# Context tokens as the stationary operand of the first FFN's matmuls, with 512 weight columns moving, in a one-layer hybrid mLSTM / spatial-gating kernel

## The chip, the cores and the metric

The kernel runs on one core of one Trainium2 chip. The metric is the device time of one execution in microseconds, as the median of several runs. Before the change it was 2650.72 us (three runs, 2648.93 to 2655.58).

The engines are called by the profile's names: PE multiplies matrices (one operand is held in the array, the other moves through it column by column), PEld loads the held operand, DVE and ACT work elementwise, POOL does a few small things, and SP issues the transfers. Each engine runs its instructions in the order in which they were put on it.

## The reference, cut to what matters

One layer works on 1024 latent tokens and 256 context tokens of width 1024. Both run through a half-step SwiGLU FFN of inner width 2816, a token-mixing part and a second FFN; the context tokens are needed only up to the mixing part.

```
def ffn_sublayer(h, shift, scale, gate, g, w_in, w_out):
    hn = modulate(rmsnorm(h, g), shift, scale)
    a, b = jnp.split(hn @ w_in, 2, axis=-1)      # 1024 -> 2 x 2816
    y = (jax.nn.silu(a) * b) @ w_out             # 2816 -> 1024
    return h + 0.5 * gate[:, None, :] * y
```

Behind the first FFN the mixing part projects the normalised tokens with one wide matrix into q, k, v, gates, o, u and others. It runs a bidirectional mLSTM of four heads over chunks of 128 tokens (whose weights hold `exp(dm - m_t)`) and a chunked spatial-gating MLP, `gelu(u)` times a 128x128 mix of the normalised `gelu(vs)`, merges the two by sigmoid gates and projects once more. Everything is fp32.

## The kernel before, in words

**Numbers and tiles.** Each fp32 operand of a large product is split into a high part (rounded to the type fp32r) and a low part (the remainder): ACT casts the high part and DVE subtracts it from the source (`split`, L145 and L146). A product is then three matmuls: high by high, high by low, low by high (`mm3`, L182). Tokens lie along the free dimension, channels along the partitions: eight tiles of 128 channels by 512 latent tokens (`h`, two token blocks) or by 256 context tokens (`hc`; normalised and split `hnc`).

**Stages.** The latent matrices use a scheme of seven half-size products in place of eight, with pages `fa`, `fb`, `fc` of combined operands. In order of time: adaLN rows (to about 37 us); the first FFN's up-projection of the context tokens (to 169); the same for the latent tokens, `A.gate` with L411 (to 588); the latent down-projection `A.outp` with L535 (to 801); the context down-projection with L1161 (to 867); `wv` by `Rows` (L1292, PSUM tile `pr`) and the context's v (`pvc`, L1451); further projections (`pq`, L1373), with the spatial-gating mix (`pm` by PE, `mx` by DVE, L1813 and L1815) and the Gelu of u among the last; four heads (from about 1577) beside the product with `w_b` (`pt`, L1853); `w_a` and `w_o`; the second FFN (2001 to the end).

**Context up-projection.** `for f in range(NF)` takes two pages of weights per f, one of the SiLU half and one of the other. Weights are held in PE, 256 context tokens move: `pa` and `pb` each take 24 matmuls of 256 columns per f. After two f, ACT takes the SiLU of `pa` (128x512), DVE multiplies by `pb`, ACT and DVE split the result, and SP stores it to DRAM (`gcsp`). The result already has channels on the partitions, as the down-projection wants it. Beside it run the position embedding, the sums of squares of the latent norm (`acc`, L209) and, from f = 10, the scaling of the latent tokens (`inplace`, L261 on DVE and L262 on ACT). At the end `A.begin` loads and splits the gate's first four weight pages into `ring`.

**Context down-projection.** Per f, each of eight channel tiles takes three matmuls of 256 columns with `wring` weights held and `gc` moving, added up in four PSUM tiles `pc`. Then DVE adds the gated result to `hc`, and the next norm of the context tokens follows: ACT squares, DVE adds (`acc`), PE sums over the partitions (`p`, L214), DVE and ACT take the inverse root (`rs_x` to `rs_y`, L758 to L764), ACT and DVE form a diagonal matrix split in two (`diag`, L224 and L225), and PE spreads it (`rb`, L230).

**What sets the order.** The order on PE, DVE and ACT is set by the program's own order and a scheduler below it. Small work is put between matmuls by hand: `todo` is a queue of functions, and `pump` takes one after each 512 columns of matmul (a `nop` there is an empty slot of 512 columns). `tc.issue_after` makes instructions come behind a named one. Weight pages and `ring` tiles live in pools: a page can be overwritten only when its last matmul is done. `ring` has four slots, so the cast of the fifth page waits for the first page's 12 matmuls, and so on.

## Time and profile before

| | us |
|---|---|
| median of three runs | 2650.72 |
| lowest, highest | 2648.93, 2655.58 |
| the profiled execution | 2650.17 |
| its span in the trace | 2648.4 |
| PE busy | 2634.0 (99%), 12904 instructions |
| DVE busy | 1946.5 (73%) |
| ACT busy | 1205.5 (46%) |
| granted PE clock, mean | 0.998 |

The span is the time from the first to the last instruction in the trace; the profiled execution's own time is 1.8 us longer. A busy PE counts the records of matmuls, which overlap: a record lasts longer than the slot that the matmul takes in a stream, so prices per matmul are read from the distance between starts, or from the chain of waits, which gives unbroken pieces with their counts.

### The profile page before, as it was taken

The page shows a single profiled execution, that of the slowest core. Times are in us where ns is not written, and L with a number is a line of the kernel's source. Part 1 is how long each engine was busy: PE and PEld are TensorE (multiplying, and loading weights), DVE is VectorE, ACT ScalarE, POOL GpSimd, SP SyncE. Part 2 cuts the span into 40 slices and gives each one's busy share as a digit, 9 for nine tenths or more (in the row PEclk, how much of TensorE's full clock was granted, in tenths as well). Part 3 has the DMA queues.
Part 4 walks back from the last instruction along what each step waited for, and adds up shares of the span by engine and source line. Part 5 has one row for each costly group of instructions (what it writes and reads, how often), then busy time and mean ns, then how long its engine had stood idle before and what let it go on. Part 6 is the DMA issues. An engine that isn't in the chain of part 4 may idle for free.

```text
span 2648.4 us, 35940 instructions
## 1 busy us (share of the span) xinstructions
PE 2634.0 (99%) x12904; PEld 2211.2 (83%) x12904; DVE 1946.5 (73%) x3490; ACT 1205.5 (46%) x2171; POOL 80.3 (3%) x158
## 2 busy tenths in 40 slices
PE   9999999999999999999999999999999999999998
PEld 6998888888889878888888888888888888888887
DVE  7988688687989646787664869777568766665755
ACT  5664444444346525564443454333256444344433
POOL 0000000000000000000000003221000000000000
PEclk9999999999999999999999999999999999999999
DMA  9834344368578222356653457547341343337654
GB/s 315 307 111 136 119 163 167 113 232 308 175 238 292 74 80 91 104 176 195 197 171 105 150 195 265 184 152 267 129 146 41 124 142 112 123 123 275 202 157 181
DMA packets 201234, 452.73 MB, mean 171 GB/s; under 512 B 20320, under 2 KB 54624, under 8 KB 201056
## 3 DMA queue, kind: packets, MB, share of 16 engines
q1 hardware_dynamic: 200624, 450.05, 50.4%
q8 instruction: 101, 1.65, 0.3%
q14 instruction: 77, 0.63, 0.1%
q10 hardware_dynamic: 432, 0.39, 0.0%
HBM read 329.11 MB, written 121.32 MB: 170 GB/s over the span
## 4 chain that ended last, share of the span: by engine, by line
PE 94%; DMA 2%; issue 2%; ACT 1%; DVE 1%; SPq 0%; POOL 0%; POOLq 0%; DVEq 0%; ACTq 0%
PE qa L411 18%; PE pq L1373 17%; PE po L535 14%; PE qb L411 14%; PE pt L1853 10%; PE pr L1292 5%; PE pa L182 2%; PE pb L182 2%; PE pc L1161 2%; PE pn L1987 2%; PE pu L1695 1%; PE pkc L1352 1%; PE pn L1985 1%; PE pvc L1451 1%; DMA adapg<-in_w_ada_dram 1%
## 5 line engine op out<-in xcount | busy, mean ns | idle before, releaser
L146 DVE TENSOR_TENSOR ring<-rawq,ring 128x512 fp32r<-128x512 f32 x408 | 281.0, 690 | 222.1 <-ACT ring L145 218.7
L535 PE MATMUL po<-gring,wring 128*128 128x512 f32 (+1 forms) x1896 | 424.0, 384 | 0.8 <-DMA gring<-fsp 0.8
L535 PEld LDWEIGHTS po<-gring,wring 128*128 128x128 f32 x1896 | 349.3, 188 | 71.5 <-ACT h L262 1.6
L145 ACT CAST ring<-rawq 128x512 fp32r<-128x512 f32 x408 | 253.3, 622 | 310.4 <-PE pq L1373 88.8
L411 PE MATMUL qa<-fc,ring 128*128 128x512 f32 x1056 | 252.3, 389 | 0.0
L411 PEld LDWEIGHTS qa<-fc,ring 128*128 128x128 f32 x1056 | 198.1, 188 | 41.5 <-DVE fc L146 0.4
L1373 PE MATMUL pq<-fc,ring 128*128 128x512 f32 x864 | 207.6, 392 | 0.0
L145 ACT CAST wring<-rw 128x512 fp32r<-128x512 f32 x154 | 95.7, 622 | 215.4 <-PE po L535 186.0
L1373 PEld LDWEIGHTS pq<-fc,ring 128*128 128x128 f32 x864 | 161.5, 188 | 33.4
L1853 PE MATMUL pt<-yp,ring 128*128 128x512 f32 x768 | 186.9, 396 | 2.3 <-DVE mx L1813 2.3
L1853 PEld LDWEIGHTS pt<-yp,ring 128*128 128x128 f32 x768 | 143.5, 189 | 31.1 <-issue 2.5
L146 DVE TENSOR_TENSOR wring<-rw,wring 128x512 fp32r<-128x512 f32 x154 | 105.6, 686 | 79.9 <-ACT wring L145 79.6
L1373 PE MATMUL pq<-fa,ring 128*128 128x512 f32 x576 | 142.4, 395 | 0.0
L1373 PE MATMUL pq<-fb,ring 128*128 128x512 f32 x576 | 138.5, 394 | 0.0
L1373 PEld LDWEIGHTS pq<-fb,ring 128*128 128x128 f32 x576 | 107.6, 188 | 23.9 <-issue 0.2
L411 PE MATMUL qa<-fa,ring 128*128 128x512 f32 x528 | 127.0, 390 | 0.0
L411 PE MATMUL qb<-fb,ring 128*128 128x512 f32 x528 | 126.5, 389 | 0.0
L411 PE MATMUL qa<-fb,ring 128*128 128x512 f32 x528 | 126.5, 390 | 0.0
L411 PE MATMUL qb<-fc,ring 128*128 128x512 f32 x528 | 126.2, 389 | 0.0
L411 PE MATMUL qb<-fa,ring 128*128 128x512 f32 x528 | 126.2, 389 | 0.0
L1373 PEld LDWEIGHTS pq<-fa,ring 128*128 128x128 f32 x576 | 106.8, 188 | 22.4 <-DVE ring L146 0.2
L793 DVE SCALAR_TENSOR_TENSOR adacc<-adapg,sc,adacc 128x512 f32<-128x512 f32 x154 | 111.9, 747 | 16.8 <-DMA adapg<-in_w_ada_dram 15.7
(364 smaller groups left out, 4652.8 us busy)
## 6 DMA issues: line engine op xcount, KB each, us to landing
adapg<-in_w_ada_dram SPq DMA_DIRECT2D x144, 256.0 KB, 3.6
fsp<-fhl SPq DMA_DIRECT2D x66, 512.0 KB, 2.7
gring<-fsp SPq DMA_DIRECT2D x66, 512.0 KB, 4.1
raw<-in_w1i_dram SPq DMA_DIRECT2D x44, 512.0 KB, 5.2
graw<-fsp SPq DMA_DIRECT2D x88, 256.0 KB, 3.7
rawq<-in_w1i_dram SPq DMA_DIRECT2D x38, 512.0 KB, 3.6
rawq<-in_w2i_dram SPq DMA_DIRECT2D x38, 512.0 KB, 3.6
fsp<-p SPq DMA_DIRECT2D x66, 256.0 KB, 2.2
```

Of the source, the lines that this page charges most:

```text
L145: hi = S.copy(hl[:, 0, :], src)
L146: return hi, V.tensor_sub(hl[:, 1, :], src, hl[:, 0, :].bitcast(F32))
L182: T.matmul(pt, x, y, start=first and i == 0, stop=i == n - 1, skip_group_check=True)
L411: T.matmul(pt, hl[:, x, sl], pages[p][k][:, y, :], start=first and i == 0, stop=i == 11, skip_group_check=not first)
L535: T.matmul(pt[:, cs], w[:, x, sl], g[:, y, cs], start=grp and kp == 0 and i == 0, stop=kp == NFP - 1 and i == 2, skip_group_check=not grp)
L793: eng.scalar_tensor_tensor(acc, pgt, sc2[:, q, k:k + 1], acc, ALU.mult, ALU.add)
L1161: T.matmul(pt, hl[d // 4][:, x, sl], g[:, y, :], start=f == 0 and d % 2 == 0 and i == 0, stop=f == NF - 1 and i == 2, skip_group_check=True)
L1292: T.matmul(self.pt[m], pg[:, x, sl], hl[:, y, :], start=first and k == 0 and i == 0, stop=k == 3 and i == 2, skip_group_check=not first)
L1352: T.matmul(self.cp[:, o:o + 256], hl[:, x, k * 128:(k + 1) * 128], hnc[kc][:, y, :], start=p == 1 and k == 0 and i == 0, stop=p in (2, 4) ...
L1373: T.matmul(pt, hl[:, x, k * 128:(k + 1) * 128], pg[k][:, y, :], start=first and k == 0 and i == 0, stop=k == 3 and i == 2, skip_group_chec ...
L1853: T.matmul(pt, hl[:, x, k * 128:(k + 1) * 128], pg[:, y, :], start=kh + k + i == 0, stop=kh == 1 and k == 3 and i == 2)
L1987: T.matmul(pn[:, 0:257], qi[:, c_, :], self.C[d][:, c_, :], start=False, stop=c_ == 1)
```

## The change

Four things change.

1. *Context up-projection.* The tokens are held and the weights move. A new layout `w1c` of the same weights has 44 pages of 128x1024, four for each of 11 blocks; a page holds two k tiles of 512 columns, of which 256 are of the SiLU half and 256 of the other. Per block, each of two token halves (`pts[0]`, `pts[1]`) takes 24 matmuls of 512 columns. `gated` takes two SiLU of 128x256 and two products; `turned` transposes the result with four PE transposes into `ptg`, splits it from there and stores it. `turned` of a block runs one page into the next block; the last is put into the gate's queue. The old work beside f is in `beside`. The scaling of the second latent block moves to the gate's queue, whose lead goes from 16 to 24.
2. *Context down-projection.* The `gc` tokens are held and 512 columns of `wring` move: 12 matmuls per f in place of 24 narrow ones. ACT and DVE copy the four `pc` to `co`; `cturn`, four times, transposes four tiles into `pct`, and DVE adds them to `hc` from there. `cturn` is queued in `todo` behind three empty slots and so runs inside `wv`.
3. *The latent down-projection.* `A.outp` gets `free`: late loads go to pages that are no longer used. In `fin1` seven empty slots, where three were, stand between the inverse root and the spread.
4. *The heads.* The first head's two exponentials are taken out of `Head` preparation into `expo`, which is issued behind the last Gelu; the split of the `w_b` operand (`yp`) is also tied behind a `mx`.

```diff
-    W = Weights([("w1i", f, 1024) for f in range(2 * NF)], "w1")
+    W = Weights([("w1c", i, 1024) for i in range(4 * NFP)], "w1")
...
-            for d in range(NKT):
-                slow(n1[1].inplace, d, s0, b0)
...
-            for pt, w_ in ((pa, wa), (pb, wb)):
-                proj(pt[:, f % 2 * 256:f % 2 * 256 + 256], w_, hnc, f % 2 == 0 and ks[0] == 0, ks)
...
+    def gated(pts, fn=None):
+        sil = t2("sil").rearrange("p (i c) -> p i c", i=2)
+        for i in range(2):
+            S.activation(sil[:, i, :], pts[i][:, 0:256], AF.Silu)
+        with ExitStack() as es:
+            if fn is not None:
+                es.enter_context(tc.issue_after(fn().ins))
+            for i in range(2):
+                V.tensor_mul(sil[:, i, :], sil[:, i, :], pts[i][:, 256:512])
+        return sil
+
+    def turned(blk, sil):
+        pt = sm_ps("ptg")
+        for j in range(2):
+            for i in range(2):
+                T.transpose(pt[:, j * 256 + i * 128:j * 256 + (i + 1) * 128], sil[:, i, j * 128:(j + 1) * 128], ident)
+        g = [t2("gc", F32R) for _ in range(2)]
+        S.copy(g[0], pt)
+        V.tensor_sub(g[1], pt, g[0].bitcast(F32))
...
+    for blk in range(NFP):
+        pts = [mm_ps("pa") for _ in range(2)]
+        for kp in range(4):
+            if kp % 2 == 0:
+                beside(2 * blk + kp // 2)
+            w_ = W.take("w1c", 4 * blk + kp)
+            for k in (2 * kp, 2 * kp + 1):
+                o = k % 2 * 512
+                for i in range(2):
+                    for n, (x, y) in enumerate(THREE):
+                        T.matmul(pts[i], hnc[k][:, x, i * 128:(i + 1) * 128], w_[:, y, o:o + 512],
+                                 start=k == 0 and n == 0, stop=k == NKT - 1 and n == 2)
+                    pump(512)
+            if kp == 0:
+                if turn is not None:
+                    turned(*turn)
...
+        turn = blk, gated(pts, first_ring if blk == NFP - 1 else None)
+    todo.extend([nop] * 4 + [it(turned, *turn)])
...
-    A.gate(A.F.late(fpage, lambda k: []), tick, 16)
+    A.gate(A.F.late(fpage, lambda k: [it(n1[1].inplace, k, s0, b0)]), tick, 24)
...
-        todo.extend([nop] * 6 + [n_.rstd, nop, nop, nop, n_.bcast])
+        todo.extend([nop] * 6 + [n_.rstd] + [nop] * 7 + [n_.bcast])
...
+           free=(lambda: ringpg("wring"), lambda kp: hnpage(1, "gring") if kp > 3 else ringraw("gring")))
...
+        for i in range(2):
+            for j in range(2):
+                for n, (x, y) in enumerate(THREE):
+                    T.matmul(pcs[2 * i + j], g[:, x, i * 128:(i + 1) * 128], hl[j][:, y, :], start=f == 0 and n == 0,
+                             stop=f == NF - 1 and n == 2)
+                pump(512)
...
+    def cturn(d2):
+        pt = sm_ps("pct")
...
+    todo.extend([nop] * 3)
+    for d2 in range(4):
+        slow(cturn, d2)
...
-            S.activation(pg, pg, AF.Exp)
...
+    with tc.issue_after(ureads[False].ins):
+        for d in range(2):
+            heads[0].expo(d)
```

What this does to the order on the engines, at three places.

ACT at the end of the context up-projection, before; `hl` are casts of its weight pages, `fb` and `h` work for the latent tokens, `sil` the SiLU of the last block, `ring` the casts of the gate's first weights:

```order
L145 CAST hl<-raw 128x1024
L1060 CAST gc<-sil 128x512
L145 CAST hl<-raw 128x1024
L145 CAST fb<-h 128x512 x3
L1052 ACTIVATE sil<-pa 128x512
L145 CAST ring<-rawh 128x512 x5
L1060 CAST gc<-sil 128x512
```

and with the change, where `gc<-ptg` is the high part of a transposed block:

```order
L145 CAST hl<-raw 128x1024
L1051 CAST gc<-ptg 128x512
L145 CAST fb<-h 128x512
L262 ACTIVATE h<-h,mods 128x512 x2
L145 CAST fb<-h 128x512 x2
L1037 ACTIVATE sil<-pa 128x256 x2
L145 CAST ring<-rawh 128x512 x4
```

In both, the last block's SiLU stands directly ahead of the gate's casts; it was one of 512 columns and is now two of 256, which need all of the block's matmuls.

PE at the start of `wv`, before; `pc` is the end of the context down-projection, `p` the sums of the context's norm, `rb` its spread, `pr` the products of `wv`:

```order
L1161 MATMUL pc<-gc,wring 128x256 x456
L1292 MATMUL pr<-ring,fa 128x512 x21
L214 MATMUL p_8226<-ones,acc 128x1 x2
L1292 MATMUL pr<-ring,fa 128x512 x24
L230 MATMUL rb<-diag,onesr 128x256
L1292 MATMUL pr<-ring,fa 128x512
L230 MATMUL rb<-diag,onesr 128x256
L1292 MATMUL pr<-ring,fa 128x512 x50
```

and with the change, where `pct` are the transposes of the down-projection's result (the last `pc` end just ahead of these rows):

```order
L1332 MATMUL pr<-ring,fa 128x512 x15
L1209 MATMUL pct<-cst,co 128x128 x4
L1332 MATMUL pr<-ring,fa 128x512 x6
L1209 MATMUL pct<-cst,co 128x128 x4
L1332 MATMUL pr<-ring,fa 128x512 x6
L1209 MATMUL pct<-cst,co 128x128 x4
L1332 MATMUL pr<-ring,fa 128x512 x6
L1209 MATMUL pct<-cst,co 128x128 x4
L1332 MATMUL pr<-ring,fa 128x512 x15
L214 MATMUL p_7581<-ones,acc 128x1 x2
L230 MATMUL rb<-diag,onesr 128x256 x2
L1332 MATMUL pr<-ring,fa 128x512 x48
```

The sums moved from behind 21 matmuls of `pr` to behind 48 (15 + 6 + 6 + 6 + 15), and between the sums and the spread, where 24 matmuls stood, there is none.

ACT at the same place, before; `ring` are casts of weight pages, `rs_z` the root, `diag` the diagonal, `rx` the copies of the first product that must be made before PE may add the second one there:

```order
L145 CAST ring<-raw_8169 128x512
L760 ACTIVATE rs_z<-rs_x 128x2
L145 CAST ring<-raw_8171 128x512
L145 CAST ring<-raw_8173 128x512
L1526 CAST wgp<-wgr 128x8x16
L224 ACTIVATE diag<-cst,rs_y 128x128 x2
L1303 COPY rx<-pr 128x512 x2
L243 ACTIVATE nt<-nt,mods 128x256
L1303 COPY rx<-pr 128x512
L244 CAST hnc<-nt 128x256
L1303 COPY rx<-pr 128x512
L145 CAST ring<-raw_8175 128x512
```

and with the change:

```order
L1202 COPY co<-pc 128x512 x2
L145 CAST ring<-raw_7431 128x512
L145 CAST ring<-raw_7433 128x512
L1564 CAST wgp<-wgr 128x8x16
L205 ACTIVATE acc<-hc 128x256
L208 ACTIVATE sq<-hc 128x256 x7
L145 CAST ring<-raw_7435 128x512
L145 CAST ring<-raw_7437 128x512
L760 ACTIVATE rs_z<-rs_x 128x2
L224 ACTIVATE diag<-cst,rs_y 128x128 x2
L1343 COPY rx<-pr 128x512 x4
```

The root and the diagonal now stand behind the fourth weight page's cast (`raw_7437`), where they stood ahead of the fourth (`raw_8175`), and all four copies come behind the diagonal.

ACT around the first head's exponentials, before; `P` are the first head's weights, L1931 their exponential, `ug` the Gelu, `yp` the casts of the operand of `w_b`:

```order
L1931 ACT_TABLE_LOAD
L1931 ACTIVATE P<-P 128x1024
L1929 ACTIVATE P<-P,colpg 128x128
L1433 ACT_TABLE_LOAD
L1433 ACTIVATE ug<-ug 128x512
L1931 ACT_TABLE_LOAD
L1931 ACTIVATE P<-P 128x1024
L145 CAST yp<-ld 128x512 x4
L145 CAST ring<-rawt 128x512
L1966 CAST kh<-ptk 128x512
L1430 ACT_TABLE_LOAD
L1430 ACTIVATE ug<-pq 128x512
```

and with the change, where L1976 is the exponential:

```order
L1967 ACTIVATE P<-P,colpg 128x128 x16
L1472 ACTIVATE ug<-ug 128x512
L145 CAST yp<-ld 128x512 x4
L1470 ACTIVATE ug<-pq 128x512
L145 CAST yp<-ld 128x512 x2
L145 CAST ring<-rawt 128x512
L145 CAST yp<-ld 128x512 x2
L145 CAST ring<-rawt 128x512
L1472 ACTIVATE ug<-ug 128x512
L1976 ACT_TABLE_LOAD
L1976 ACTIVATE P<-P 128x1024 x2
```

Both exponentials moved behind the casts of `yp` and the last Gelu, and three of the four table loads shown before are gone.

More of the change, by code (lines that the diff above doesn't have):

```diff
@@ L1014, in slow, with beside @@
         todo.append(f)
-    for f in range(NF):
+    def beside(f):
         if 0 < f <= NKT:
@@ L1034, in _build @@
             A.preload()
-        wa = W.take("w1i", 2 * f)
-        wb = W.take("w1i", 2 * f + 1)
-        if f % 2 == 0:
-            pa, pb = mm_ps("pa"), mm_ps("pb")
-        for ks in (range(6), (6, 7)) if f == 0 else (range(NKT),):
-            for pt, w_ in ((pa, wa), (pb, wb)):
-                proj(pt[:, f % 2 * 256:f % 2 * 256 + 256], w_, hnc, f % 2 == 0 and ks[0] == 0, ks)
-                if f == 0 and ks[0] == 0 and pt is pa:
+    def gated(pts, fn=None):
[8 more added lines that the diff above has]
+        return sil
@@ new lines, in first_ring @@
+    def first_ring():
+        flush()
+        W.c.close()
+        A.begin()
+        return A.q.last[1]
+    turn = None
+    for blk in range(NFP):
[14 more added lines that the diff above has]
+                    turned(*turn)
+                else:
@@ L1043, in _build @@
                     last0()
-                if ks[-1] == NKT - 1:
-                    W.done()
-        if f == 0:
+            W.done()
+        if blk == 0:
             order.close()
-        if f % 2 == 0:
-            continue
-        with ExitStack() as es:
-            sil = t2("sil")
-            S.activation(sil, pa, AF.Silu)
-            if f == NF - 1:
-                flush()
-                W.c.close()
-                A.begin()
-                es.enter_context(tc.issue_after(A.q.last[1].ins))
-            V.tensor_mul(sil, sil, pb)
-            g = [t2("gc", F32R) for _ in range(2)]
-            S.copy(g[0], sil)
-            V.tensor_sub(g[1], sil, g[0].bitcast(F32))
```

51 lines of the change are left out of this document (29 added, 22 removed).

## The prediction

> **What bounds the kernel now.** I read the page's busy shares first, then PE's list of waits, then the chain of waits with its times, then the stretches that the change touches.
>
> ```profile
> PE 2634.0 (99%) x12904; PEld 2211.2 (83%) x12904; DVE 1946.5 (73%) x3490; ACT 1205.5 (46%) x2171; POOL 80.3 (3%) x158
> PE pt L1853 <- DVE mx L1813: 2.3, 1, 2.3
> PE po L535 <- DMA gring<-fsp: 0.8, 2, 0.5
> PE rb L230 <- ACT diag L224: 0.6, 1, 0.6
> 50.69 2.88 PE pa L182 x24
> 245.14 5.44 PE qa L411 x24
> 812.42 54.72 PE pc L1161 x456
> 50.50:169.00 118.50, 118.50 (x983) 118.04 (x982) 107.83 (x163) 81.96 (x118) 0.00 (x0) 1.00 0.75 257
> 108.30:119.80 11.50, 11.50 (x98) 11.50 (x97) 11.49 (x15) 10.15 (x15) 0.00 (x0) 1.00 0.80 265
> ```
>
> PE is busy for 2634.0 of the span's 2648.4 us: 14.4 us are idle in all, and the list of waits names the few that are long. So PE's own stream is the bound nearly everywhere, a transfer or a slow engine costs only where PE stands still, and each PE matmul saved or added counts in full. The chain gives the prices of one matmul in an unbroken stream: 256 columns 54.72/456 = 0.120 us, 512 columns 5.44/24 = 0.2267 us. Two of the first cost 0.240, so a wide one that does the work of two saves 0.0133 us. The last two rows are stretches (start:end, length, busy time of PE, weight load, DVE, ACT with counts): the first FFN's context part has DVE at 107.83 of 118.50 us, and in the stretch from 108.30 at 11.49 of 11.50. DVE is second there, and close.
>
> **Part 1, context up-projection (36.7 to 168.8).** Its matmuls are counted by these rows of the line's view (count: shortest/median/longest ns, first to last start), and L1161 is the context down-projection.
>
> ```profile
> L182 PE MATMUL pa<-hnc,hl x528: 278/283/386, 36.7 to 165.8; 128*128 128x256 f32 x176
> L1161 PE MATMUL pc<-gc,wring x528: 278/283/363, 801.4 to 866.9; 128*128 128x256 f32 x176
> 1651.23 1.53 PE L2017 MATMUL pth<-cst,hm 128*128 128x128 f32 x12
> 1652.52 0.48 PE L1853 MATMUL pt<-yp,ring 128*128 128x512 f32 x1
> ```
>
> 528 + 528 matmuls of pa and pb make 1056 x 0.120 = 126.7 us; 528 of the wide form make 528 x 0.2267 = 119.7: **-7.0**. New are 44 transposes of 128x128. The trace has such ones in another stage: 12 fill 1651.23 to 1652.52, 0.107 us each, so 44 x 0.107 = **+4.7**.
>
> The transposes stand in PE's row, one page (12 matmuls, 2.72 us) into the next block, and what they read comes through ACT and DVE. Prices:
>
> ```profile
> 166.11 0.60 ACT L1052 ACTIVATE sil<-pa 128x512 f32<-128x512 f32 x1 [0.59 <-PE pa L182]
> 166.61 2.17 ACT L145 CAST ring<-rawh 128x512 fp32r<-128x512 f32 x4
> 167.25 2.50 DVE L146 TENSOR_TENSOR ring<-rawh,ring 128x512 fp32r<-128x512 f32 x4 [1.00 <-ACT ring L145]
> 168.79 8.35 PE L411 MATMUL qa<-fa,ring 128*128 128x512 f32 x36
> L145 ACT CAST hl<-raw 128x1024 fp32r<-128x1024 f32 x43 | 45.0, 1048 | 33.4 <-PE pa L182 15.0 <-PE pb L182 7.6 <-issue 5.5
> L146 DVE TENSOR_TENSOR hl<-raw,hl 128x1024 fp32r<-128x1024 f32 x44 | 53.5, 1220 | 5.7 <-ACT hl L145 5.5
> 865.56 1.65 DVE L1174 SCALAR_TENSOR_TENSOR hc<-pc,hgate,hc 128x256 f32<-128x256 f32 x4
> ```
>
> Half the columns of the 0.60 SiLU are about 0.40 (an estimate). After a block's end T: 0.2 until ACT starts (pa ends 24 x 0.12 after its start at 163.03, at 165.91, and SiLU starts at 166.11), SiLU 0.40, a page's cast 1.05 that ACT's order puts between, second SiLU 0.40: T+2.05. DVE has the page's low part (1.22) from about T+1.7, then the second product (1.65/4 = 0.41): T+3.3. PE wants it after 12 matmuls, one transpose and one more matmul, at T+3.05. That is a wait of 0.2 in most blocks; some blocks give the products more room, so I take **+1.5** over 10 blocks. Ends: 0, if DVE runs ahead, and 12, if one more DVE item of 1.2 us stands in front in each (first rival).
>
> The last block hands over to the gate. Before, both SiLU and the four casts of the gate's first weights ran while PE did the last page of pb (2.88 us), and L411 at 168.79 follows pb without a gap. Now pa and its gate half end together with the block, and ACT has two SiLU ahead of those casts: 0.2 + 2 x 0.40 + 0.62 for one cast is T+1.6, and its low part on DVE (2.50/4, 0.63) comes at T+2.3 for the second matmul, wanted 0.23 after the first. That is 1.6 to 2.0; I take **+1.7**, ends 1.2 and 2.5. The latent scaling (eight in-place pairs of one block) is only queued later; the order shows most of it still in this stage, off PE: 0. Sum of part 1: +0.9.
>
> **Part 2, the output projection's end.**
>
> ```profile
> 783.08 7.66 PE L535 MATMUL po<-gring,wring 128*128 128x512 f32 x33
> 791.01 2.55 PE L535 MATMUL po<-gring,wring 128*128 128x512 f32 x10 [0.27 <-DMA gring<-fsp]
> 794.08 7.50 PE L535 MATMUL po<-gring,wring 128*128 128x512 f32 x32 [0.52 <-DMA gring<-fsp]
> 807.26 3.71 PE L1161 MATMUL pc<-gc,wring 128*128 128x256 f32 x29
> 811.53 0.50 PE L230 MATMUL rb<-diag,onesr 128*128 128x512 f32 x1 [0.55 <-ACT diag L224]
> ```
>
> By slots of 0.2267, 33 matmuls from 783.08 end at 790.56, and 10 from 791.01 at 793.28: gaps of 0.45 and 0.80 us, both on the loads of gring. Those now go to freed pages, earlier: **-1.2** (ends 0 and -1.25). The spread of the norm (L230) sits 29 matmuls behind its sums; 29 x 0.12 from 807.26 ends at 810.74, so PE stood for 0.79. The four more empty slots put 24 wide ones (5.4 us) there, over the 4.3 that the answer took: **-0.8** (ends 0 and -0.8).
>
> **Part 3, context down-projection and what follows.** 528 x 0.120 - 264 x 0.2267 = **-3.5**; 16 transposes at 0.107 = **+1.7**. Both are certain as counts. The norm behind it moves, though, into the next stage (wv, pr), and there I find the largest loss.
>
> ```profile
> 871.80 0.50 PE L214 MATMUL p<-ones,acc 128*128 128x1 f32 x4
> 872.17 5.73 PE L1292 MATMUL pr<-ring,fa 128*128 128x512 f32 x24
> 872.34 0.16 DVE L758 TENSOR_SCALAR rs_x<-p 128x2 f32<-128x2 f32 x1 [0.83 <-PE p L214]
> 873.68 0.16 DVE L764 SCALAR_TENSOR_TENSOR rs_y<-rs_z,rs_x 128x2 f32<-128x2 f32 x1
> 875.94 0.62 ACT L145 CAST ring<-raw 128x512 fp32r<-128x512 f32 x1 [2.12 <-PE pr L1292]
> 876.59 0.69 DVE L146 TENSOR_TENSOR ring<-raw,ring 128x512 fp32r<-128x512 f32 x1 [2.05 <-ACT ring L145]
> 876.66 0.69 ACT L224 ACTIVATE diag<-cst,rs_y 128x128 fp32r<-128x128 f32 x2
> 877.26 1.05 ACT L1303 COPY rx<-pr 128x512 f32<-128x512 f32 x2
> 877.73 0.28 PE L230 MATMUL rb<-diag,onesr 128*128 128x256 f32 x1
> ```
>
> Before, the sums (L214) come after 21 matmuls and the spread (L230) 24 matmuls later, so PE works while DVE and ACT compute. In the changed order the sums come after all 48 of the first product, the spread directly behind, and the next 48 need ACT's copies (L1303) of that product. Ahead of the last sum DVE has the low part of a weight page whose cast waits for the 48th matmul to free its slot (call its end E). In these rows a cast starts 0.37 after the matmul it waits for (21 before the sums and 15 behind 872.17 make the 36th of the stage, which ends at 875.57; the cast starts at 875.94). So: E+0.37 cast, DVE from 0.65 later to E+1.7, accumulation 0.41, sums at E+2.1, L758 0.54 behind them (871.80 to 872.34), L764's end 1.50 later (E+4.1), the first diag 0.39 (half of the 0.69 row and its start), spread at E+4.6, then ACT's copy 0.59 and the product at E+5.3. PE does 0.3 us of work in it: **+5.0** idle (ends 2.5, the chain from the sums alone, and 5.6).
>
> What an idle PE costs beyond that stands in the stretch around the kernel's longest wait, at 1581.4:
>
> ```profile
> 1581.40:1583.70 2.30, 0.00 (x0) 0.03 (x1) 2.30 (x5) 0.92 (x2) 0.00 (x0) 1.00 0.87 243
> 1584.00:1585.00 1.00, 1.00 (x5) 0.78 (x4) 1.00 (x3) 0.17 (x1) 0.00 (x0) 0.72 0.99 381
> 1586.00:1587.00 1.00, 1.00 (x5) 0.66 (x5) 1.00 (x2) 0.99 (x3) 0.00 (x0) 0.50 0.93 262
> 1588.00:1589.00 1.00, 1.00 (x6) 0.80 (x6) 1.00 (x3) 1.00 (x3) 0.00 (x0) 1.00 0.00 0
> 1578.20 1.06 ACT L1931 ACTIVATE P<-P 128x1024 f32<-128x1024 f32 x1
> 1576.90 1.28 ACT L1931 ACT_TABLE_LOAD   x1
> ```
>
> The column before the last two is the granted clock. After 2.30 us without a matmul it falls to 0.50 from about 1584.4 to 1587.7, 3.3 us in which half the work is done: 1.7 us lost on top of the wait. A wait of 5.0 is longer, so I add **+1.5** (ends 0.6 and 2.3, by where the stretch at half clock begins). The Trainium skill, page "TensorE: Matmul & The Clock Gate", section "What's actually happening", says that the gate halves the clock after an idle window of about 3.4 us and gives it back after a busy one. The trace agrees on the half and the length, 3.3 us, but 2.3 us of idleness were enough; by the rule to the letter the new wait would pay the same.
>
> **Part 4, the first head's exponentials.** Each is a table load (1.28) and 1.06 us on ACT, ahead of the casts that the first pt needs; DVE is late by them, and the wait of 2.3 follows. Both now come after the last Gelu, behind those casts. I take 2.0 of the 2.3 and the 1.7 at half clock: **-3.7** (ends 0 and -4.0). Later readers of P come well after.
>
> **Sum**: 0.9 - 1.2 - 0.8 - 3.5 + 1.7 + 5.0 + 1.5 - 3.7 = -0.1. The profiled execution took 2650.17 (span 2648.4), the median of the three runs is 2650.72; half way, 2650.4 - 0.1 is about **2650**.
>
> **Rivals.** *Transposes late in every block (slower).* In-order PE stands at ten sets of transposes until DVE has multiplied; DVE full at 11.49 of 11.50 us speaks for it, the weight pages held ahead against it. It decides as soon as the product ends later than 2.95 us after the block. One more low part ahead is 1.2 x 10 = 12, less the 1.5 counted: 2650 + 10.5 = 2660.5. Chance 0.12.
>
> *The wait in wv does not arise (faster).* If the sums' inputs are ready at E, PE loses nothing there: -6.5, and with a handover of 0.6 another -1.1: 2642.4. For it: all hc work ends 3 us ahead of E. Against: the cast named above stands before it on ACT and DVE. Chance 0.12.
>
> *The moved orders do not do what they say*: gring loads still late, spread still early, pt waiting for another DVE item: +1.2 + 0.8 + 3.7 = 5.7, 2655.7. The 2.3 wait had two DVE items behind the casts, which speaks a little for it. Chance 0.10.
>
> *Transposes do not pipeline.* Each takes its whole record of about 0.283 (the median in the rows of part 1) rather than its slot: 60 x 0.176 = +10.6, 2660.6. The 12 in 1.29 us speak against it; none of those stands behind an fp32r stream of 12. Chance 0.03. The Trainium skill, same page, section "Part 4: PE-mode transpose", has about 275 ns for one in a kernel's context; by it the 60 would cost 16.5, not 6.4, and the result would be near this rival's. The rows of this trace, 107 ns, do not agree.
>
> **Numbers.** The forecast, 2650, keeps 0.63. Within 0.3% (7.95 us) a measurement of this kernel cannot be told from no change. Faster: the second rival, 0.12, lies just beyond that bound, and I give 0.12 in all; slower: 0.12 + 0.03 = 0.15; the same: 0.73. Range 2642 to 2658: the ends of the large terms (-4 for wv, +4 for the transposes' waits) and both smaller rivals.
>
> **What would show it.** A page of 12 in 2.72 us; waits of PE on the transposes' products near 0.2 each; 1.2 to 2 us idle before L411's first matmul; about 5 us idle around L214 and L230 at the start of wv with a clock of 0.50 behind it; no wait of po on gring, none of pt on mx, full clock near 1584. It is wrong if that idle stretch is missing, or if DVE's products hold PE for over 0.5 us a block.

## The result, and the profile after

| | before | changed |
|---|---|---|
| median of 13 runs each, us | 2653.04 | 2659.32 |
| lowest, highest | 2648.93, 2656.6 | 2656.19, 2662.6 |
| the profiled execution | 2650.17 | 2659.32 |
| its span | 2648.4 | 2657.2 |

The changed kernel takes 1.0022 times as long, with a 95% interval of [1.0014, 1.0029]. It is slower by some 6 us, 1.3 us above the range's upper end. That is under the 0.3% within which the prediction said no change could be told, but the interval does tell it from none. (The prediction started from 2650.4; over 13 runs the kernel before lies at 2653.04.)

Cut at landmarks that both traces have, the two profiled executions (one of each kernel) differ so. The last column is a version with four mends, told of below.

| stage, us | before | changed | mended |
|---|---|---|---|
| start to the first context matmul | 36.73 | 37.41 | 36.96 |
| to the gate's piece of 72 `qb` (context up-projection) | 140.41 | 144.13 | 140.70 |
| to the first `pc` (latent gate and `A.outp`) | 624.28 | 623.12 | 622.99 |
| to the first `pr` (context down-projection) | 65.56 | 61.27 | 61.27 |
| to the `pr` behind `pvc` (start of `wv`) | 44.45 | 52.94 | 46.91 |
| to the piece of 384 `pq` | 171.20 | 171.20 | 171.20 |
| to the piece of 534 `pt` (heads) | 755.89 | 757.14 | 753.56 |
| to the end | 809.88 | 809.99 | 810.51 |

So +3.7 in the context up-projection, -1.2 and -4.3 in the next two stages, +8.5 in `wv`, +1.3 at the heads: with +0.7 ahead of the first matmul the difference of the spans, 8.8. The line numbers below are those of the changed kernel's source.

The busy shares of the changed kernel, and from PE's list of waits (who waited, for whom, us in total, times, longest) its entries of 0.5 us or more:

```profile
PE 2635.2 (99%) x12172; PEld 2177.2 (82%) x12172; DVE 1950.2 (73%) x3503; ACT 1204.2 (45%) x2180; POOL 77.2 (3%) x158
PE pt L1891 <- ACT ring L145: 2.0, 1, 2.0
PE p L214 <- DVE acc L209: 1.9, 1, 1.9
PE rb L230 <- ACT diag L224: 1.9, 1, 1.9
PE ptg L1049 <- DVE sil L1042: 1.9, 3, 1.0
PE pu L1733 <- DVE C L1734: 1.8, 2, 1.2
...
PE qa L411 <- ACT ring L145: 1.0, 1, 1.0
PE pa L1075 <- DVE hl L146: 1.0, 2, 0.8
```

Where the list of before had one long wait, this one has five entries of about 2 us (those of `ptg` and `pu` are sums of shorter waits), and three of them are new: the transposes (`ptg`), the sums (`p`) and the spread (`rb`) of the context's norm. The wait of `pt` was to vanish, and stands there with another releaser.

**The context up-projection.** From the changed kernel's timeline (start, length, instruction, idle time before it) the first pages, one set of transposes, and the end, where ACT's two SiLU stand ahead of the gate's casts:

```profile
46.62 5.72 PE L1075 MATMUL pa<-hl,hnc 128*128 128x512 f32 x24 [0.76 <-DVE hl L146]
...
103.51 0.60 PE L1049 MATMUL ptg<-cst,sil 128*128 128x128 f32 x4
103.86 3.70 PE L1075 MATMUL pa<-hl,hnc 128*128 128x512 f32 x15
...
170.91 0.38 ACT L1037 ACTIVATE sil<-pa 128x256 f32<-128x256 f32 x1 [0.97 <-PE pa L1075]
171.59 0.38 ACT L1037 ACTIVATE sil<-pa 128x256 f32<-128x256 f32 x1 [0.29 <-PE pa L1075]
172.53 2.64 PE L411 MATMUL qa<-fa,ring 128*128 128x512 f32 x10 [0.98 <-ACT ring L145]
```

Four transposes take 0.35 us from their first start to the next product's, 0.0875 each. The wait at 46.62 is one of three for weight pages in the first 10 us; before there was one, of 0.2. PE is idle for 0.98 ahead of the gate's first matmul (172.53); counted from start to start this one comes 1.14 late (records outlast their slots). The chain of waits shows why the transposes at 78.52 are late:

```profile
75.99 0.41 DVE sil L1042
76.40 0.60 DVE acc L209
77.00 1.14 DVE hl L146
78.14 0.34 DVE sil L1042
78.52 0.56 PE ptg L1049 x3
```

Between the two products DVE does not only the page's low part, as the prediction had it, but also a sum of squares of the latent norm. Two more late sets, at 66.56 and 90.59, have the same sum there; in the fourth, at 140.07, it is the combining of the gate's first weights (0.68), behind a load for which DVE had waited 1.05 us.

**The output projection's end.** In the timeline of PE `A.outp` now ends in one piece without a gap, and the spread follows 24 wide matmuls at once:

```profile
787.64 17.18 PE L535 MATMUL po<-gring,wring 128*128 128x512 f32 x75
810.23 5.75 PE L1188 MATMUL pc<-wring,gc 128*128 128x512 f32 x24
```

**The start of wv.** The timeline of PE, ACT and DVE (rows between left out):

```profile
875.19 3.69 PE L1332 MATMUL pr<-ring,fa 128*128 128x512 f32 x15
...
878.92 0.62 ACT L145 CAST ring<-raw 128x512 fp32r<-128x512 f32 x1 [0.74 <-PE pr L1332]
...
879.66 0.69 DVE L146 TENSOR_TENSOR ring<-raw,ring 128x512 fp32r<-128x512 f32 x1
880.26 0.42 DVE L209 TENSOR_TENSOR acc<-acc,sq 128x256 f32<-128x256 f32 x1
880.83 0.58 PE L214 MATMUL p<-ones,acc 128*128 128x1 f32 x4 [1.94 <-DVE acc L209]
...
882.56 0.69 ACT L224 ACTIVATE diag<-cst,rs_y 128x128 fp32r<-128x128 f32 x2 [0.72 <-DVE rs_y L764]
...
883.30 0.78 PE L230 MATMUL rb<-diag,onesr 128*128 128x256 f32 x2 [1.90 <-ACT diag L224]
883.91 0.82 PE L1332 MATMUL pr<-ring,fa 128*128 128x512 f32 x2
```

The 15 matmuls end at 878.59, and the next product starts at 883.91: the cast of the fourth page, its low part, the sum, the inverse root and the diagonal stand in a row, in the order that the prediction gave. With E for the end of the 15, the cast starts at E+0.33 (predicted 0.37), its low part ends at 1.76 (1.7), the sums start at 2.24 (2.1), the spread at 4.71 (4.6) and the product at 5.32 (5.3). In stretches of 3.41 us (start:end, length, busy time of PE, weight load, DVE, ACT, POOL, granted clock, DMA):

```profile
877.36:880.77 3.41, 1.53 (x7) 0.94 (x5) 3.11 (x7) 1.44 (x3) 0.00 (x0) 1.00 0.00 0
880.77:884.18 3.41, 1.45 (x8) 1.15 (x9) 1.52 (x8) 1.83 (x6) 0.00 (x0) 1.00 0.00 0
884.18:887.60 3.42, 3.42 (x10) 2.64 (x9) 1.94 (x4) 2.62 (x7) 0.73 (x1) 0.50 0.02 5
```

The clock is 0.50 for the whole third stretch, which costs 1.7.

**The heads.** SP's queue around the first `pt`, before (`ld` loads the operand of `w_b`, `rawt` its weights):

```profile
1569.89 5.01 SPq L1889 DMA_DIRECT2D ld<-ybsp  x5
1574.94 0.42 SPq L1862 DMA_DIRECT2D rawt<-in_w_b_dram  x1
```

and in the changed kernel, with the rows of ACT and PE that follow:

```profile
1577.25 8.29 SPq L1927 DMA_DIRECT2D ld<-ybsp  x8
1585.59 0.42 SPq L1900 DMA_DIRECT2D rawt<-in_w_b_dram  x1
...
1589.43 0.62 ACT L145 CAST ring<-rawt 128x512 fp32r<-128x512 f32 x1 [0.24 <-DMA rawt<-in_w_b_dram]
1590.11 6.23 PE L1891 MATMUL pt<-yp,ring 128*128 128x512 f32 x19 [2.01 <-ACT ring L145]
```

The exponentials are out of the way, as intended. But the first weight page was behind five loads on SP, and is now behind eight, the last three of which wait until DVE's splits (`yp`) free their slots. It is asked for 4.5 us ahead of the first `pt`, where that was 8.8, and its cast at 1589.43 waits for it. PE stood for 2.0 us, and the clock fell once more:

```profile
1587.33:1590.74 3.41, 1.40 (x10) 1.06 (x9) 0.79 (x3) 2.92 (x6) 0.00 (x0) 1.00 0.75 249
1590.74:1594.16 3.42, 3.42 (x10) 2.68 (x9) 3.28 (x7) 2.06 (x4) 0.00 (x0) 0.50 0.46 161
```

A little further on, in both kernels behind the same 48 `pt`, 16 `ptk` and 32 `sp`, PE reaches the first product `pn` of the heads (before, then changed):

```profile
1597.77 0.60 PE L1985 MATMUL pn<-v,P 128*128 128x257 f32 x2
1605.16 0.67 PE L2028 MATMUL pn<-v,P 128*128 128x257 f32 x2
```

From the piece of 384 `pq`, which starts at 1082.63 and 1090.07, that is 515.14 and 515.09 us: up to there the new order gained nothing and lost nothing. (The five other traces with this order, of runs 3 to 7, have 514.6 to 516.5.) The stage's +1.3 lies behind it, where PE's waits of `pu` for DVE's `C` are 1.8 us for 0.8. Over the thirteen traces these waits come to between 0.7 and 3.7 us, with the code of `pu` the same in all, so this part can be scatter.

### The profile page after: what moved, and what is told of

It reads as the page before. It is cut to its first block, busy times and chain, and to the rows that moved or that the text cites. A ratio compares the mean times of both kernels' runs of the same rounds, so it can differ in the third digit from the quotient of the medians.

```text
span 2657.2 us, 34506 instructions
## 1 busy us (share of the span) xinstructions
PE 2635.2 (99%) x12172; PEld 2177.2 (82%) x12172; DVE 1950.2 (73%) x3503; ACT 1204.2 (45%) x2180; POOL 77.2 (3%) x158
## 4 chain that ended last, share of the span: by engine, by line
PE 92%; DVE 3%; DMA 2%; issue 2%; ACT 1%; POOL 0%; SPq 0%; POOLq 0%; DVEq 0%; ACTq 0%
PE qa L411 18%; PE pq L1413 17%; PE po L535 15%; PE qb L411 14%; PE pt L1891 9%; PE pr L1332 5%; PE pa L1075 3%; PE pc L1188 2%; PE pn L2030 2%; PE pu L1733 1%; PE pn L2028 1%; PE pkc L1392 1%; PE pvc L1489 1%; DMA P<-srow 1%; PE pu L1771 1%
## 5 line engine op out<-in xcount | busy, mean ns | idle before, releaser
L1891 PEld LDWEIGHTS pt<-yp,ring 128*128 128x128 f32 x768 | 144.1, 190 | 30.8 <-ACT ring L145 2.2
L1075 PE MATMUL pa<-hl,hnc 128*128 128x512 f32 x528 | 126.2, 394 | 1.5 <-DVE hl L146 1.0
```

The costliest lines, as they stand in the source:

```text
L1075: T.matmul(pts[i], hnc[k][:, x, i * 128:(i + 1) * 128], w_[:, y, o:o + 512], start=k == 0 and n == 0, stop=k == NKT - 1 and n == 2)
L1891: T.matmul(pt, hl[:, x, k * 128:(k + 1) * 128], pg[:, y, :], start=kh + k + i == 0, stop=kh == 1 and k == 3 and i == 2)
```

## The experiments

Theory: the loss is made of separate waits, each with one cause, and each can be taken away alone: the norm's chain in `wv`, the transposes, the handover, the late weight page at the heads. The rival for each: the loss lies in the wide form itself, or moves on when a wait is mended. Ratios are to the kernel before, run beside each set (medians 2652.95, 2652.8 and 2653.01); the changed kernel's is 1.0022 [1.0014, 1.0029].

**1. The exponentials back where they were** (`e1_m4_undone`): the first head's two exponentials are again in its preparation, and the splits of `yp` are tied as before.

```diff
-            if h_:
-                self.expo(d)
+            self.expo(d)
...
-    with tc.issue_after(ureads[True].ins), tc.issue_after(ureads["m"].ins):
+    with tc.issue_after(ureads[True].ins):
         page_splits(yb, early)
-    with tc.issue_after(ureads[False].ins):
-        for d in range(2):
-            heads[0].expo(d)
```

> The changed kernel with only the order of the heads taken back: both exponentials of the first head stand ahead of the yp casts again, and the yp split is not tied behind mx. Theory A (the wait only changed its cause: the load of the first w_b piece, rawt, now stands behind eight loads of ld on SP in place of five, so the edit gained nothing): 2659 us within 1.5 of the changed kernel, pt waits 2 to 2.6 us on mx as before, the clock falls to 0.50 behind it, and SP issues rawt behind five ld. Theory B (the edit is worth the 3.7 us that I predicted, and the loss is elsewhere): 2663.

Measured: 2659.12, ratio 1.0023 [1.0014, 1.0032], as with the edit. The edit by itself gained nothing. `pt` waited 2.6 us for `mx`, as in the kernel before, yet the clock stayed full. In stretches of 3.41 us at this place:

```profile
1586.99:1590.40 3.41, 1.88 (x17) 1.64 (x16) 2.85 (x5) 3.09 (x7) 0.00 (x0) 1.00 0.32 88
1590.40:1593.82 3.42, 2.19 (x10) 1.47 (x10) 3.42 (x7) 1.23 (x1) 0.00 (x0) 1.00 0.78 262
```

The wait lies across an edge of two stretches here, 1.5 us idle in the one and 1.2 in the other. In the kernel before the 2.3 us lay in one. So this execution was spared the 1.7 by luck; for how many of the ten that holds is not known.

**2. The first weight page of pt ahead of later loads** (`e2_rawt_ahead`): the last four of the eight loads `ld` are issued a step later.

```diff
             page_splits(yb, page_loads(ybsp, (0, 1)))
+        elif i == 8:
             early.extend(page_loads(ybsp, (2, 3)))
```

> The changed kernel with the loads of the second four ld issued one step later, so that SP issues the first rawt behind four ld. Theory A (SP's order is what holds pt): PE's wait at the first pt falls from 2.0 to below 0.5 us, the granted clock stays 1.00 there, and the time falls by 3 to 4 us, to about 2655.5. Theory B (the yp casts or mx are as late as rawt): the wait only changes its name and the time stays within 1 us of 2659.

Measured: 2656.93, ratio 1.0014 [1.0005, 1.0022]. SP asked for the page at 1580.73. `pt` still waited, 1.4 us and not under 0.5, and the heads' stage took 755.82 for 757.14. The page's cast stands on ACT behind four casts of `yp`, and the first pair of these waited 0.9 us for its loads, which took 5.3 us from the first one's issue to the cast. The time is 2.4 us less, and by its interval not apart from the changed kernel's.

**3. The norm's steps spread out in wv** (`e3_wv_gap`): the sums come six matmuls later, when what they read is ready, and 21 matmuls stand between sums and spread.

```diff
-    nct.queue(smod[:, 1, 1, :], mods[:, 3, 1, :], hnc, gap=(1, 2, 8), cost=1280)
+    nct.queue(smod[:, 1, 1, :], mods[:, 3, 1, :], hnc, gap=(5, 6, 0), cost=1280)
```

> The changed kernel with the sums of the context norm four empty slots later and the spread seven slots behind them (five and six empty slots where one and two stood), so that 21 matmuls stand between the sums and the spread and the copies of the first wv product come ahead of the root on ACT. Theory A (sums, root, spread and copies in a row with no matmul between them are the loss at the start of wv): the idle 4.9 us there fall below 1.5, the clock stays 1.00, the context's v waits up to 2 us longer for hnc, and the time falls by 3 to 6 us, to about 2654.5. Theory B (the chain is bound by the weight page's cast, and moving it only moves the wait to the context's v): within 1.5 us of 2659.

Measured: 2652.87, ratio 1.0001 [0.9992, 1.001]: 6.4 us less than the changed kernel, its interval apart from that one's. The stage took 46.90 for 52.94. PE's timeline of this run:

```profile
875.05 5.19 PE L1332 MATMUL pr<-ring,fa 128*128 128x512 f32 x21
880.22 0.58 PE L214 MATMUL p<-ones,acc 128*128 128x1 f32 x4
880.66 5.03 PE L1332 MATMUL pr<-ring,fa 128*128 128x512 f32 x21
885.52 0.40 PE L230 MATMUL rb<-diag,onesr 128*128 128x256 f32 x2
```

No idle time before any of them. All of the chain's work is still done, under 21 matmuls, and the clock stays at 1.00. One line took back as much as the change had lost; what is left of its losses (part 1, the transposes in `wv`) and its gains (`A.outp`, the down-projection) is level in the medians.

**4. The transposes one page later** (`e4_turn_later`): 24 matmuls instead of 12 ahead of them.

```diff
-            if kp == 0:
-                if turn is not None:
-                    turned(*turn)
-                else:
-                    last0()
+            if kp == 0 and turn is None:
+                last0()
+            if kp == 1 and turn is not None:
+                turned(*turn)
```

> The changed kernel with each block's four transposes two pages (24 matmuls) into the next block where they stood one page in. Theory A (PE stands at the transposes because the second product of DVE is later than one page): PE's waits on sil, 3.8 us over the ten blocks by the distances of PE's starts, fall below 0.5, and the time falls by 3 to 4 us, to about 2656. Theory B (DVE is the limit of this stage, and what PE does not wait at the transposes it waits at the weight pages): PE's sum of idle in 37 to 172 us stays within 1 us and the time within 1 us of 2659.

Measured: 2657.39, ratio 1.0014 [1.0005, 1.0023]. The waits of `ptg` are gone from the list, and the stage took 141.29 for 144.13, 2.8 less. The medians differ by 1.9; in this profile `pt` waited 2.5 us where it had waited 2.0. The stage is shown, the time alone would not show it. The other traces agree: the six with the wide up-projection and the transposes one page in have 144.1 to 147.0 us there, the four with them two pages in 140.6 to 141.3.

**5. The context up-projection of before** (`e5_up_old`), with its layout and its loop over f; everything else as changed:

```diff
-    W = Weights([("w1c", i, 1024) for i in range(4 * NFP)], "w1")
+    W = Weights([("w1i", f, 1024) for f in range(2 * NF)], "w1")
```

> The changed kernel with the context up-projection alone as before (256 columns moving, nothing transposed, its SiLU one page before the end); all else is the change. Theory A (wide matmuls save 7.0 us there, transposes cost 4.7, PE's waits at them 3.8 and the handover to the gate 1.5, so this part lost about 3): the gate is reached some 3 to 4 us sooner and the time is about 2656. Theory B (my prediction's sum, +0.9 for this part): within 1.5 us of 2659.

Measured: 2656.69, ratio 1.0014 [1.0005, 1.0023]. The stage is back at 140.78 (before: 140.41). So part 1 of the change costs 3.4 us, in that stage (the stage of run 4, with the transposes later, is nearly back as well).

**6. The context down-projection of before** (`e6_down_old`), with the norm's place that goes with it; the rest as changed:

```diff
-        for i in range(2):
-            for j in range(2):
-                for n, (x, y) in enumerate(THREE):
-                    T.matmul(pcs[2 * i + j], g[:, x, i * 128:(i + 1) * 128], hl[j][:, y, :], start=f == 0 and n == 0,
...
-    for d2 in range(4):
-        slow(cturn, d2)
```

> The changed kernel with the context down-projection alone as before (256 columns moving, nothing transposed, sums after 21 matmuls of wv and the spread 24 behind them). Theory A (this part saves 3.5 us of stream and pays 1.7 for transposes, 4.9 of idle and 1.2 to 1.5 of half clock at the start of wv, and some 0.7 in the context's v): 4 to 5 us faster than the changed kernel, about 2654.5, with no idle of PE over 0.5 us there and the clock at 1.00. Theory B (the idle there is made up later, as PE's gains in the heads' stage were): within 1.5 us of 2659.

Measured: 2653.38, ratio 1.0003 [0.9994, 1.0012], 5.9 less than the changed kernel. Its stage from the first `pr` took 44.37 as before. This and run 3 give the same time by opposite means: one keeps the wide matmuls and moves the norm, the other goes back to the narrow ones. It is the norm's place and not the wide form that cost. (The execution that was profiled is this run's slowest. Its up-projection, with the code of the changed kernel, took 146.96: the waits at the transposes came to 3.1 us, the longest 1.5, and the clock fell to 0.50 after that one.)

**7. The gate's first casts ahead of the last block's SiLU** (`e7_ring_first`): both SiLU move into the scope that ties instructions behind these casts. In the trace the first still runs ahead of the casts and the second behind them.

```diff
-        for i in range(2):
-            S.activation(sil[:, i, :], pts[i][:, 0:256], AF.Silu)
         with ExitStack() as es:
             if fn is not None:
                 es.enter_context(tc.issue_after(fn().ins))
             for i in range(2):
+                S.activation(sil[:, i, :], pts[i][:, 0:256], AF.Silu)
+            for i in range(2):
```

> The changed kernel with the gate's first four casts tied ahead of the last block's second SiLU on ACT. The wait of PE for ring at the start of the gate is 1.0 us, 1.3 by the starts, and 1.5 with the second matmul's. Theory A (the SiLU in front of the casts is its cause): one SiLU less in front takes 0.4 us off, the rest stays because the first SiLU and a cast still follow the block's end, and the time is 2659 within 1 us. Theory B (the casts wait for something else): the 1.0 stays as it is.

Measured: 2658.42, ratio 1.0022 [1.0012, 1.0031]. PE's wait at the handover fell from 0.98 to 0.30 us, 0.7 where 0.4 was expected: the casts no longer wait for the second token half either, whose SiLU started 0.68 behind the first. It is too little for the time to show.

**8. The mends of 2, 3, 4 and 7 together** (`e8_all`).

> The changed kernel with four mends together: the transposes two pages into the next block, the gate's first casts ahead of the second SiLU, the wv sums and spread later, and the first rawt load ahead on SP. If the parts add up: 3.0 (transposes, by the stage) + 0.4 + 6.4 + 1.3 to 2.4 less than 2659.3, so 2647 to 2648.5, which would be 0.2% faster than before. If PE's gains ahead of the heads are lost again in the heads' stage, where the waits depend on transfers, 2650 or more.

Measured: **2646.41** (2644.41 to 2647.74), ratio 0.9976 [0.9967, 0.9985]: faster than both kernels, 6.4 below the one before and 12.9 below the changed one, and a little under the sum of the parts. SP and PE of this run at the heads:

```profile
1567.34 1.90 SPq L1926 DMA_DIRECT2D ld<-ybsp  x4
1569.28 0.48 SPq L1899 DMA_DIRECT2D rawt<-in_w_b_dram  x1
1575.20 3.89 PE L1890 MATMUL pt<-yp,ring 128*128 128x512 f32 x14 [0.37 <-ACT ring L145]
```

The weight page is asked for behind four loads, and PE waits 0.4 us, at full clock. The heads' stage is 753.56, 2.3 less than before the change, and 2.3 less than in run 2, which has the same two edits at this place; runs 9 and 11 show a part of why.

**9 to 11. One piece of before in the mended version.** Is each part of the change worth something once its wait is gone? In run 9 the context up-projection is that of before, in run 10 the order of the exponentials (the diff of run 1), in run 11 the context down-projection with its norm (the diff of run 6, without that of run 3).

> The version with the four mends (2646.41), but with the context up-projection of the kernel before, so neither late transposes nor a late handover are in it. Theory A: with the transposes one page later the wide up-projection still only breaks even, since its first stage took 140.70 us there and 140.78 us where the old up-projection stood: 2645.7 to 2647.7. Rival B: the count decides (7.0 us fewer columns against 44 transposes at 0.09 us, 4.0 us): this is slower by about 3.0, 2649.4.

> The version with the four mends (2646.41), but with the first head's exponentials ahead of the last Gelu as in the kernel before. Theory A: moving them is worth something as soon as the first load of the weights of pt no longer stands behind the eight loads of its operand: the heads' stage goes back from 753.6 to about 756.4 us, a wait of pt on the Vector engine's mx near 2 us is back, time 2648.5 to 2649.7. Rival B: the early load alone made the gain, the exponentials are neutral: 2645.7 to 2647.2.

> The version with three of the mends (the gap in wv is not needed here), with the context down-projection of the kernel before and its norm hidden in wv as there. Theory A: once its norm is hidden the wide down-projection is worth its count, 3.5 us of columns less 16 transposes at about 0.1 us: this is slower than 2646.41 by 1.5 to 2.5, 2648 to 2649. Rival B: the transposes and their copies give the gain back: 2645.7 to 2647.2.

Measured, beside 0.9976 [0.9967, 0.9985] with all parts:

| | median | ratio |
|---|---|---|
| 9, old up-projection | 2647.74 | 0.9984 [0.9975, 0.9992] |
| 10, old order of the exponentials | 2649.37 | 0.9986 [0.9978, 0.9995] |
| 11, old down-projection | 2648.00 | 0.9979 [0.997, 0.9988] |

The intervals overlap, and run 8 was measured in another set: by the ratios runs 9, 10 and 11 are 2.1, 2.7 and 0.8 us slower than it, by the medians 1.3, 3.0 and 1.6. So the stages have to tell. Run 9: the up-projection's stage takes 140.80 us, with the new one 140.70. Theory A holds for the stage; the time settles neither, as the median is just outside A's numbers and 1.7 below B's 2649.4. That profiled execution lost its time at the heads instead (759.17; the run's range is 2645.88 to 2654.65). Run 11 has the same code there and 753.84. Ahead of the first `pt` the timelines of both, 9 first, show one difference:

```profile
1567.87 1.89 SPq L1934 DMA_DIRECT2D ld<-ybsp  x4
1573.12 1.29 ACT L145 CAST yp<-ld 128x512 fp32r<-128x512 f32 x2 [2.10 <-DMA ld<-ybsp]
1576.74 0.50 PE L1898 MATMUL pt<-yp,ring 128*128 128x512 f32 x1 [1.37 <-ACT ring L145]
```

```profile
1567.83 1.92 SPq L1912 DMA_DIRECT2D ld<-ybsp  x4
1572.18 1.29 ACT L145 CAST yp<-ld 128x512 fp32r<-128x512 f32 x2 [0.81 <-DMA ld<-ybsp]
1575.80 1.39 PE L1876 MATMUL pt<-yp,ring 128*128 128x512 f32 x4 [0.48 <-ACT ring L145]
```

The loads of the operand are issued at the same time and taken up after 5.3 us in run 9, after 4.4 in run 11; PE waits 1.4 and 0.5. The rest of the 5.3 us between the two stages lies further on: a wait of 0.7 at `ptk`, waits of `pu` of 3.7 us for 1.3, and a fall of the clock behind them in run 9 (1.7). Run 2 had 5.3 and 1.4, run 8 4.2 and 0.4. With the page early, then, the landing of these loads sets the start of `pt`, and it differs by about 1 us between executions. What they share the DMA engines with at that moment was not tried.

Run 10: the time is that of theory A. The heads' stage takes 758.2, which does not tell, as the four traces with both edits (2, 8, 9, 11) have 753.6 to 759.2. And the wait came at another place than I expected, at the transposes `ptk` and not at `pt`:

```profile
1582.14 0.41 PE L2005 MATMUL ptk<-cst,kT 128*128 128x128 f32 x2 [3.16 <-DVE P L1997]
```

Run 11: from the first `pc` to the `pr` behind `pvc` it is 109.05 us against 108.18. The wide down-projection is worth 0.9 in the profiles and 1.6 in the medians, at the low edge of theory A. B is not excluded by the times.

## Why the prediction was wrong, step by step

| term | predicted | in the profiles |
|---|---|---|
| wide matmuls of the up-projection | -7.0 | -6.9 |
| its 44 transposes | +4.7 | +3.9 |
| PE's waits at them | +1.5 | +2.8 |
| handover to the gate | +1.7 | +1.1 |
| first pages of the weights | none | +1.8 |
| rest of that stage | none | +1.0 |
| `A.outp` | -1.2 | -1.2 |
| spread behind it and down-projection's matmuls | -4.3 | -4.3 |
| `wv`: transposes, idle PE, half clock | +8.2 | +8.5 |
| first `pt`, to the first `pn` | -3.7 | 0.0 |
| rest of the heads' stage | none | +1.3 |
| start and end | none | +0.8 |
| sum | -0.1 | +8.8 |

The two rows called rest, and start and end, are remainders of the stages, without a cause shown; one execution of each kernel is compared.

**The step that failed is part 4: "I take 2.0 of the 2.3 and the 1.7 at half clock".** I followed `pt` back to DVE and ACT, and found what the change takes out of their way. I did not follow its other operand, the weights, back to SP. There the change moves three loads ahead of the first page: the releaser is now ACT's cast of `rawt`, the wait 2.0 for 2.3, the clock falls as before, and PE reaches the first `pn` after 515.09 us for 515.14. The term is 0 and not -3.7, the largest part of the 8.9 by which the sum was off.

The runs show that the step was short of two conditions. One is the page. With the exponentials moved and the page early (2, 8, 9, 11) PE waits 1.4, 0.4, 1.4 and 0.5 at the first `pt`; with the exponentials moved alone, in six traces (the changed kernel and runs 3 to 7), 1.5 to 2.5; with the page early alone 3.2, at `ptk` (10); with neither 2.6 (1). The other is the landing of the operand's loads: from the first one's issue to its cast the traces with the exponentials moved have 4.2 to 5.6 us, and the wait grows with it. At 4.2 to 4.4 it is 0.4 and 0.5 with the page early, 1.5 and 1.7 with it late; at 5.2 to 5.3 it is 1.4 twice, and 2.0 and 2.2. So the page's place is worth 0.6 to 1.2 us of the wait; what sets the landing stays open. Even with both edits the gain up to the first `pn` is 2.5, 2.0, 0.3 and 0.0 (runs 8, 11, 9, 2; an estimate, as six more `pt` stand ahead of it there, taken off at 0.2267 each), never 3.7. The third rival had `pt` waiting for something else, at 0.10; it named a DVE item where it was the weights, and its other two parts did not come.

**Mis-sized: PE's waits at the transposes,** 1.5 against 2.8 (from run 4, 144.13 less 141.29). The chain of ACT and DVE was right, but I filled DVE's row with this stage's page only. In three blocks the latent norm's sum (0.60) stands between the two products, in one the combining of the gate's weights (0.68), and four sets come 0.3 to 1.2 us late, counted by starts, instead of all by 0.2. The first rival named this mechanism and made it too large, one item of 1.2 in every block. (It wants the product at 2.95 us, the sum above it at 3.05; it leaves out a transpose of 0.107.)

**Missing: the first pages.** Three waits on the casts and low parts of the first weights, by starts 1.8 us more than before. The trace of before has one such wait of 0.2. I priced the steady state and left out the start.

**Right: the chain in wv,** to 0.15 us at each step, and the half clock behind it, 1.7 for 1.5. Run 3 shows that it was one chain: 6.4 us, 6.0 of them in the stage. The second rival (the wait does not arise) is out. `A.outp`, the late spread and the two counts of matmuls came as predicted; the handover came out at 1.1, a little under its lower end of 1.2. The transposes cost 0.088 us each where I took 0.107 from another stage. The Trainium skill, page "TensorE: Matmul & The Clock Gate", section "Part 4: PE-mode transpose", has about 275 ns. That agrees with the length of one such record here (0.27 us at 138.81) and not with the slot that a transpose takes in a stream, and the rival near it is out.

The base was off too: the forecast started from 2650.4, and 13 runs put the kernel before at 2653.04. That is 2.6 of the 9.3 us between forecast and result; the change itself is 6.3 by the medians (8.8 by the two profiled executions, of which the one before was 2.9 below its median).

## What to carry to other kernels

When an order is changed to free one operand of a late instruction, follow every operand back to its queue, the loads on SP too: the wait goes to whichever is next, and an edit that is worth nothing alone can gain beside another (2 to 3 us here by the times of runs 8 and 10, though their intervals overlap). A reduction whose chain runs through three engines needs matmuls between its steps on PE; moving the product in front of it moved the cover away, and one line gave it back. Price a change of layout at its start and its handover as well as in its steady state: here both together (1.8 and 1.1) took what the wider matmuls gave, less their transposes (3.0).

## What the runs showed of the hardware

**When the clock falls depends on where a wait lies, not on its length alone.** Every stretch at 0.50 inside the program is 3.41 us long in these traces, or twice that, and in the changed kernel the two begin at 884.18 and 1590.74, 207 times 3.413 us apart. PE was idle for about 2.0 us of the 3.41 ahead of each. In the kernel before the wait of 2.3 us lay in one such stretch:

```profile
1581.02:1584.44 3.42, 1.11 (x7) 0.80 (x6) 3.42 (x7) 1.30 (x3) 0.00 (x0) 1.00 0.78 232
1584.44:1587.85 3.41, 3.41 (x11) 2.38 (x10) 3.41 (x7) 3.01 (x5) 0.00 (x0) 0.50 0.68 228
```

In run 1 a longer wait, 2.6 us, lay across an edge, 1.5 and 1.2, and the clock stayed at 1.00. Over the thirteen traces no stretch at full clock with up to 1.7 us idle was followed by the half clock, every one with 1.93 or more was, and between those both occur (1.84 was, 1.88 was not). How the grid lies to the program differs from trace to trace, so a wait of 2.3 us cost 1.7 more in one and a wait of 2.6 us nothing more in another; some of the scatter between runs of one kernel can come from there, though no run was made to show that. The Trainium skill, page "TensorE: Matmul & The Clock Gate", section "What's actually happening", has an idle window of about 3.4 us. The length agrees; idle it need not be, some 1.9 us of the 3.41 were enough.
